# Picking the sixteen largest scores inside the query loop of a product-key mixer

## Chip, cores, metric

One Trainium2 chip, one core of it. The metric is the time of one execution on the device, in microseconds (us); lower is better. The engines are named as in the profile: PE (TensorE matmul), PEld (its weight loads), DVE (VectorE), ACT (ScalarE), POOL (GpSimd, which here also issues the indirect DMAs) and SP (which issues most plain DMAs).

## What is computed

One layer of a hybrid decoder for 1024 prompt tokens and 64 sample tokens, width 1024: RMSNorm, an input projection, retention and RWKV-7 mixing, an output projection, then a PEER product-key mixer, a gated per-layer embedding and a last RMSNorm. The change lies in PEER:

```python
q = (xb @ wq).reshape(PEER_BLOCK, PEER_HEADS, 2, PEER_DKEY // 2)
s = jnp.einsum('phcd,hcnd->phcn', q, keys).astype(jnp.float32)   # 8 heads x 2 halves x 128 scores
sv, si = lax.top_k(s, PEER_TOPK)                                  # 16 largest of each head half
cand = sv[:, :, 0, :, None] + sv[:, :, 1, None, :]
cv, ci = lax.top_k(cand.reshape(PEER_BLOCK, PEER_HEADS, PEER_TOPK * PEER_TOPK), PEER_TOPK)
e = (jnp.take_along_axis(si[:, :, 0], ci // PEER_TOPK, axis=-1) * PEER_NKEYS
     + jnp.take_along_axis(si[:, :, 1], ci % PEER_TOPK, axis=-1))
gsm = jax.nn.softmax(cv, axis=-1)
hval = jnp.einsum('pd,phkd->phk', xb, u_tab[e])
act = (jax.nn.gelu(hval.astype(jnp.float32), approximate=False) * gsm).astype(xb.dtype)
return jnp.einsum('phk,phkd->pd', act, v_tab[e])                  # 16384 experts
```

Each token has 16 head halves with 128 scores each; of every half the 16 largest are found, and of their sums the 16 best pairs of each of 8 heads, so 128 experts for a token.

## The kernel before

Tokens are cut into nine tiles: 0 to 7 are 128 prompt tokens each, tile 8 the 64 sample tokens. PEER is done in two ways. The tiles E0 = 0, 1, 8 and G1 = 2, 3 are *gathered*: for each of a tile's 128 expert slots (64 for tile 8, whose tokens fill the partitions twice) POOL issues an indirect DMA that fetches one row of 4 KB for each of 128 partitions into a buffer `grow` (L1127), and DVE multiplies it with the token's row and sums (L1141, first table, `in_pu`) or scales and adds it to `gacc` (L1155, second table, `in_pv`). These steps form one long chain, tile after tile. The tiles G2 = 4 to 7 are *dense*: all 16384 experts are multiplied on PE (`hidden`, L1256; `dense`, L1285), and a matrix of gate weights, made by `gates` (L1227) out of one-hot tiles `oh` (DVE L1242, ACT L1244, PE `pwt` L1247, ACT L1248), picks out the 128 that count.

A product of f32 quality is made of three float32r matmuls (`mm3`, L323: high x high, high x low, low x high), so each weight tile is first split in a high part (ACT, L297) and a low part (DVE L299 or POOL L301).

The program is written in one order, and a scheduler that simulates the engines turns it into one fixed instruction list for each engine: what was written earlier goes first when it is ready in the simulation. On the chip each engine works through its list in order, waiting on semaphores.

Written in this order, around the change:

1. `early` (L1211): queries, picks and gathers of E0, advanced a step at a time while the mixers run. What is left of it is written after the joint query (`run(early)`, L1489).
2. `c_query` (L1005), the joint query of G1 and G2: for each of the 16 head halves `hc` the query weights are loaded (`wqr`, L1012) and split (`wqh`, `wql`, L1015: low part on DVE for even `hc`, on POOL for odd), the projection `pq` of G1 (256 tokens) and of G2 (512 tokens) is made by 24 matmuls each, copied to `qT` (L1023), multiplied with the keys (`psc`, L1026), and the scores are copied to the tile `ss` (L1027). `ss` holds two halves and has one buffer for each of the two groups; after each odd `hc` it is written to DRAM (`sd`, L1030, six DMAs on ACT's queue for two halves).
3. `topk` (L1033) for each tile: the scores of all 16 halves are read back in one DMA (`s`, L1038, one buffer), and for each half five DVE instructions find the 16 largest and their places (L1043 to L1047). Then come the candidate sums, the second pick of 16 out of 50 for each of 8 heads (L1069 to L1073), and the look-up of the expert numbers (L1082 DVE, L1083 POOL, L1084 DVE).
4. The loop L1509: step `i` writes `topk` of the i-th tile of G2 alternately with `gates` of the tile before, then a fifth of 96 `hidden` blocks. `topk` and `gather` of tile 2 follow in step 1, those of tile 3 in step 4.
5. `dense_fused` and `dense_stored` (L1307, L1326), and then `ple` (L1373), which ends the program tile by tile in the order E0, G2, G1; a gathered tile's result comes back from DRAM there (`py`, L1390).

Of the kernel before, what the change touches and what calls it, by code (L numbers as in the profile page):

```python
# [8 lines left out]
F32 = mybir.dt.float32  # L9
# [3 lines left out]
U32 = mybir.dt.uint32  # L13
AF = mybir.ActivationFunctionType
# [164 lines left out]
G1 = [2, 3]  # L179
# [11 lines left out]
G2 = [4, 5, 6, 7]  # L191
RSTART = 2
RRATE = 1
ERATE = 1
QB = 4
EB = 150
SIZE = {t: (64 if t == 8 else 128) for t in range(9)}


def spans(tiles):  # L200

    e = [sum(SIZE[t] for t in tiles[:i]) for i in range(len(tiles) + 1)]
    return dict(zip(tiles, e)), e[-1]
# [8 lines left out]
class K:  # L212
# [434 lines left out]
    def group_b(self, tiles, early):  # L647
# [3 lines left out]
        with ExitStack() as e:  # L651
# [12 lines left out]
            for i, t in enumerate(tiles + [None]):  # L664
# [4 lines left out]
                while live or cur is not None:  # L669
# [9 lines left out]
                    for _ in range(ERATE if E0[1] in self.rowed else 0):  # L679
                        if steps < EB:  # L680
                            steps += 1
# [13 lines left out]
    def rw_mix(self, t):  # L695
# [282 lines left out]
        if t == 7:  # L978
            self.tail = self.ep0.tile([128, 512], F32, name="tail", tag="Wq", bufs=QB)
            nc.vector.tensor_tensor(self.tail, xf, p, op=OP.mult)  # L980
# [24 lines left out]
    def c_query(self, wp, da, parts):  # L1005

        nc, I = self.nc, self.I
        for hc in range(16):
            kT = wp.tile([128, 128], F32, name="keysT")
            nc.sync.dma_start(kT, I['keysT'][:, hc])  # L1010
            raw = da.tile([128, 8, 128], F32, name="wqr", tag="uraw", bufs=UB)
            nc.sync.dma_start(raw, I['wq'][hc])  # L1012
            wh = da.tile([128, 8, 128], F32R, name="wqh", tag="uh", bufs=DW)
            wl = da.tile([128, 8, 128], F32R, name="wql", tag="ul", bufs=DW)
            self.split(wh, wl, raw, "g" if hc % 2 else "v")  # L1015
            if hc % 2 == 0:
                st = [wp.tile([128, len(tiles), 2, 128], F32, name=f"ss{tiles[0]}", bufs=1) for tiles, _ in parts]
            for (tiles, x), s in zip(parts, st):
                off, n = spans(tiles)
                p = self.ps("pq", "b")  # L1020
                self.mm3(p[:, :n], lambda k: wh[:, k, :], lambda k: wl[:, k, :], lambda k: x[0][:, k], lambda k: x[1][:, k], 8)
                qT = wp.tile([128, n], F32, name=f"qT{tiles[0]}", bufs=1)
                nc.scalar.activation(qT, p[:, :n], AF.Copy)  # L1023
                p = self.ps("psc", "a")
                for i, t in enumerate(tiles):
                    nc.tensor.matmul(p[:SIZE[t], i * 128:i * 128 + 128], qT[:, off[t]:off[t] + SIZE[t]], kT, start=True, stop=True)  # L1026
                nc.scalar.activation(s[:, :, hc % 2], p[:, :len(tiles) * 128].rearrange("p (t k) -> p t k", k=128), AF.Copy)  # L1027
                if hc % 2:
                    for i, t in enumerate(tiles):
                        nc.scalar.dma_start(self.sd[t][:SIZE[t], hc - 1:hc + 1], s[:SIZE[t], i])  # L1030
            yield

    def topk(self, tp, t, s=None, tags={}, ce=None):  # L1033
        nc = self.nc
        n = SIZE[t]
        if s is None:
            w = tp.tile([128, 16, 128], F32, name="s", bufs=1)
            nc.sync.dma_start(w[:n], self.sd[t][:n])  # L1038
            s = [w[:, j] for j in range(16)]
        sv = tp.tile([128, 16, 16], F32, name="sv")  # L1040
        si = tp.tile([128, 16, 16], U32, name="si")
        for hc in range(16):
            nc.vector.max(sv[:n, hc, 0:8], s[hc][:n])  # L1043
            nc.vector.max_index(si[:n, hc, 0:8], sv[:n, hc, 0:8], s[hc][:n])
            nc.vector.match_replace(s[hc][:n], sv[:n, hc, 0:8], s[hc][:n], -3.0e38)
            nc.vector.max(sv[:n, hc, 8:16], s[hc][:n])
            nc.vector.max_index(si[:n, hc, 8:16], sv[:n, hc, 8:16], s[hc][:n])  # L1047
            yield
        sf = tp.tile([128, 8, 2, 16], F32, name="sf")
        nc.vector.tensor_copy(sf[:n].rearrange("p h c k -> p (h c) k"), si[:n])  # L1050
        nc.vector.tensor_scalar(sf[:n, :, 0], sf[:n, :, 0], 128.0, None, op0=OP.mult)
# [120 lines left out]
    def early_query(self, wp, t, wtag, wbufs, stags):  # L1172
# [31 lines left out]
        for j in range(2):  # L1204
            s.append(wp.tile([128, 8, 128], F32, name="es", tag=stags[j], bufs=QB if stags[j] == "Wq" else 1))
            nc.sync.dma_start(s[j][:n], self.sd[t][:n, 8 * j:8 * j + 8])
        yield
        ce = wp.tile([128, 2, 8, 50], F32, name="ce", tag="Wq", bufs=QB)
        yield from self.topk(wp, t, [s[j // 8][:, j % 8] for j in range(16)], dict(eq=dict(tag="xT")), (ce[:, 0], ce[:, 1]))

    def early(self, wp):  # L1211
# [4 lines left out]
        for t in E0[1:]:  # L1216
            while t not in self.rowed:
                next(g, None)
                yield
            for _ in self.early_query(wp, t, "Wq", QB, ("Wq", "xT")):  # L1220
                next(g, None)
# [200 lines left out]
    def build(self):  # L1422
# [3 lines left out]
        with self.es:  # L1426
# [21 lines left out]
            self.ep0 = ep0 = sb("early", ee, side="right")  # L1448
            self.layout(ep0, [("V", [128, D], F32, 2), ("W", [128, D], F32, 1), ("xy", [128, D], F32, 1), ("Wq", [128, D], F32, QB), ("xT", [128, D], F32, 1)])
            early = self.behind(self.early(ep0), PE_)  # L1450
# [4 lines left out]
            for _ in a:  # L1455
                for _ in range(IE):
# [3 lines left out]
            em.close()  # L1460
            cq = sb("cq", ew, bufs=2, side="right")
            parts = [G1, G2]
            self.layout(cq, [(f"ss{g[0]}", [128, len(g), 2, 128], F32, 1) for g in parts] +
                        [(f"qT{g[0]}", [128, spans(g)[1]], F32, 1) for g in parts])
            cn = sb("cn", ew, side="right")
            c1 = sb("cx1", ew, side="right")
# [2 lines left out]
            x = self.rows_of(cx, G2)  # L1469
            da = sb("dna", eg, bufs=2)  # L1470
            self.layout(da, [("uh", [128, 8, 128], F32R, DW), ("ul", [128, 8, 128], F32R, DW), ("uraw", [128, 8, 128], F32, UB)])
            tp = sb("tk", et)
            self.e12 = {}
            n3 = spans(G2[:-1])[1]
            query = self.c_query(cq, da, [(G1, x1), (G2, x)])
# [78 lines left out]
```

## Time and profile before

| what | value |
|---|---|
| median of 3 runs (lowest to highest) | 3917.6 us (3916.54 to 3927.6) |
| profiled execution | 3925.23 us, span 3923.2 us |
| busy share | PE 86%, DVE 77%, PEld 71%, POOL 60%, ACT 31% |
| mean granted PE clock | 0.875 |
| memory traffic | 279 GB/s over the span |

A row of the profile gives line, engine, operation, the tiles written and read, shapes and a count, then busy us, mean ns of one, and the idle time of that engine just before such instructions with what ended it. PE's busy time counts overlapping matmuls once, and a matmul's duration is longer than the distance to the next one.

### The profile page before, as it was taken

The page shows a single profiled execution, that of the slowest core. Times are in us where ns is not written, and L with a number is a line of the kernel's source. Part 1 is how long each engine was busy: PE and PEld are TensorE (multiplying, and loading weights), DVE is VectorE, ACT ScalarE, POOL GpSimd, SP SyncE. Part 2 cuts the span into 40 slices and gives each one's busy share as a digit, 9 for nine tenths or more (in the row PEclk, how much of TensorE's full clock was granted, in tenths as well). Part 3 has the DMA queues.
Part 4 walks back from the last instruction along what each step waited for, and adds up shares of the span by engine and source line. Part 5 has one row for each costly group of instructions (what it writes and reads, how often), then busy time and mean ns, then how long its engine had stood idle before and what let it go on. Part 6 is the DMA issues. An engine that isn't in the chain of part 4 may idle for free. (4 is left out here: it accounts for less than half of the span.)

```text
span 3923.2 us, 52738 instructions
## 1 busy us (share of the span) xinstructions
PE 3364.1 (86%) x17749; PEld 2766.9 (71%) x17749; DVE 3004.0 (77%) x5892; ACT 1225.6 (31%) x2247; POOL 2342.8 (60%) x2051
## 2 busy tenths in 40 slices
PE   8789995777869868875998899998799989899969
PEld 7688994545747756754887777787688767677757
DVE  4454487877896798876579999998877877888765
ACT  4232221111111111211322445678523333333322
POOL 5263175554364465554577778885588778887720
PEclk9799995667877658776999999999799999999989
DMA  7266558899778878888997788888999999999952
GB/s 256 68 226 207 169 198 276 273 303 307 226 243 278 297 257 273 294 300 311 321 350 259 241 289 291 326 313 327 335 342 344 333 354 357 370 367 348 327 177 72
DMA packets 465096, 1098.81 MB, mean 280 GB/s; under 512 B 74491, under 2 KB 183289, under 8 KB 459386
## 3 DMA queue, kind: packets, MB, share of 16 engines
q0 software_dynamic: 165888, 604.05, 43.9%
q1 hardware_dynamic: 237502, 389.07, 30.4%
q10 hardware_dynamic: 61436, 102.33, 7.0%
q8 instruction: 141, 2.31, 0.2%
q14 instruction: 129, 1.06, 0.1%
HBM read 992.98 MB, written 102.24 MB: 279 GB/s over the span
## 5 line engine op out<-in xcount | busy, mean ns | idle before, releaser
L1127 POOL DMA_INDIRECT grow<-in_pv,eid x576 | 573.5, 996 | 536.7 <-DVE gacc L1155 342.6
L1127 POOL DMA_INDIRECT grow<-in_pu,eid x576 | 573.9, 996 | 452.3 <-DVE grow L1141 277.8
L1155 DVE SCALAR_TENSOR_TENSOR gacc<-grow,ac,gacc 128x1024 f32<-128x1024 f32 x571 | 731.9, 1282 | 73.3 <-DMA grow<-in_pv,eid 68.8
L1141 DVE SCALAR_TENSOR_TENSOR grow<-grow,gacc 128x1024 f32<-128x1024 f32 x576 | 691.5, 1212 | 121.4 <-DMA grow<-in_pu,eid 100.7
L1300 PE MATMUL py<-ah,vl 128*128 128x512 f32 x1024 | 405.9, 402 | 31.7 <-POOL vl L301 31.4
L1300 PE MATMUL py<-ah,vh 128*128 128x512 f32 x1024 | 409.2, 400 | 18.2 <-ACT vh L297 18.1
L328 PE MATMUL ph<-cx,ul 128*128 128x512 f32 x1024 | 407.1, 398 | 9.2 <-POOL ul L301 9.2
L326 PE MATMUL ph<-cx,uh 128*128 128x512 f32 x1024 | 408.7, 399 | 7.0 <-ACT uh L297 5.3
L327 PE MATMUL ph<-cx,uh 128*128 128x512 f32 x1024 | 407.4, 398 | 0.0
L1300 PE MATMUL py<-al,vh 128*128 128x512 f32 x1024 | 405.1, 396 | 0.0
L301 POOL TENSOR_TENSOR vl<-vraw,vh 128x640 fp32r<-128x640 f32 (+2 forms) x224 | 325.6, 1459 | 42.7 <-ACT vh L297 36.7
L301 POOL TENSOR_TENSOR ul<-uraw,uh 128x1024 fp32r<-128x1024 f32 x128 | 307.9, 2406 | 35.2 <-ACT uh L297 32.8
L297 ACT ACTIVATE vh<-vraw 128x640 fp32r<-128x640 f32 (+2 forms) x224 | 154.8, 693 | 373.6 <-PE py L1300 165.5
L1300 PEld LDWEIGHTS py<-ah,vl 128*128 128x128 f32 x1024 | 193.3, 189 | 95.0 <-POOL vl L301 52.8
L1300 PEld LDWEIGHTS py<-ah,vh 128*128 128x128 f32 x1024 | 194.4, 190 | 77.1 <-ACT vh L297 36.5
L1304 DVE TENSOR_TENSOR yT<-yT,py 128x512 f32<-128x512 f32 x216 | 147.4, 684 | 121.7 <-PE py L1300 121.4
L328 PEld LDWEIGHTS ph<-cx,ul 128*128 128x128 f32 x1024 | 196.3, 192 | 51.4 <-POOL ul L301 10.9
L326 PEld LDWEIGHTS ph<-cx,uh 128*128 128x128 f32 x1024 | 196.1, 191 | 48.8 <-ACT uh L297 6.5
L327 PEld LDWEIGHTS ph<-cx,uh 128*128 128x128 f32 x1024 | 196.2, 192 | 40.3
L1300 PEld LDWEIGHTS py<-al,vh 128*128 128x128 f32 x1024 | 193.8, 189 | 43.1
L1247 PE MATMUL pwt<-oh,oh 128*128 128x128 f32 x1024 | 162.0, 310 | 63.2 <-ACT oh L1244 53.8
L1247 PEld LDWEIGHTS pwt<-oh,oh 128*128 128x128 f32 x1024 | 149.7, 213 | 84.7 <-ACT oh L1244 74.0
(401 smaller groups left out, 7815.1 us busy)
## 6 DMA issues: line engine op xcount, KB each, us to landing
uraw<-in_puT SPq DMA_DIRECT2D x128, 512.0 KB, 5.0
vraw<-in_pvd SPq DMA_DIRECT2D x152, 320.0 KB, 5.9
cw<-in_w_out SPq DMA_DIRECT2D x128, 256.0 KB, 5.5
wd<-wst ACTq DMA_DIRECT2D x28, 1024.0 KB, 15.4
wt<-wd SPq DMA_DIRECT2D x64, 448.0 KB, 7.5
wraw<-in_w_ret SPq DMA_DIRECT2D x48, 512.0 KB, 5.0
ewq<-in_wq SPq DMA_DIRECT2D x48, 512.0 KB, 5.5
gd<-geh ACTq DMA_DIRECT2D x96, 256.0 KB, 4.9
```

The lines of the kernel that those rows point to most:

```text
L297: nc.scalar.activation(hi, src, AF.Copy)
L301: nc.gpsimd.tensor_tensor(lo, src, hi.bitcast(F32), op=OP.subtract)
L326: mm(out, lh(k), rh(k), start=first and k == 0, stop=False)
L327: mm(out, lh(k), rl(k), start=False, stop=False)
L328: mm(out, ll(k), rh(k), start=False, stop=last and k == nk - 1)
L1127: nc.gpsimd.indirect_dma_start(out=g, out_offset=None, in_=src, in_offset=bass.IndirectOffsetOnAxis(ap=self.eid[t][:, j:j + 1], axis=0))
L1141: nc.vector.scalar_tensor_tensor(g[:, c], g[:, c], 1.0, x[:, c], op0=OP.mult, op1=OP.mult, accum_out=hv[:, i, j:j + 1])
L1155: nc.vector.scalar_tensor_tensor(y[:, c], g[:, c], ac[:, j:j + 1], y[:, c], op0=OP.mult, op1=OP.add)
L1247: nc.tensor.matmul(pw[:, j, :], oh[1][:, j, :], oh[0][:, j, :], start=True, stop=True)
L1300: nc.tensor.matmul(p, lh[:, b, :], rh, start=b == 0 and j == 0, stop=b == nb - 1 and j == 2)
L1304: nc.vector.tensor_tensor(yT[:, d, :], yT[:, d, :], p, op=OP.add)
```

## The change

`c_query` keeps one head half in an `ss` tile, with SB = 3 buffers for each group instead of one of double size. Right after the copy of the scores it runs the five pick instructions for each of the six tiles on `ss` (new method `pick`) and writes values and places into two tiles `sv`, `si` for each token tile (`self.found`), made before the query in the pool `tk`. The DMAs to `sd` are gone for these tiles. `topk` of the six tiles starts from `self.found`: it has no read-back, and its sixteen pick steps, each of which gave way to `gates`, are gone. The low part `wql` is made on POOL for every `hc`. For E0 nothing changes but the place of the five lines.

```diff
+SB = 3
@@ c_query
-            self.split(wh, wl, raw, "g" if hc % 2 else "v")
-            if hc % 2 == 0:
-                st = [wp.tile([128, len(tiles), 2, 128], F32, name=f"ss{tiles[0]}", bufs=1) for tiles, _ in parts]
-            for (tiles, x), s in zip(parts, st):
+            self.split(wh, wl, raw, "g")
+            for tiles, x in parts:
                 off, n = spans(tiles)
+                s = wp.tile([128, len(tiles), 128], F32, name=f"ss{tiles[0]}", bufs=SB)
...
-                nc.scalar.activation(s[:, :, hc % 2], p[:, :len(tiles) * 128].rearrange("p (t k) -> p t k", k=128), AF.Copy)
-                if hc % 2:
-                    for i, t in enumerate(tiles):
-                        nc.scalar.dma_start(self.sd[t][:SIZE[t], hc - 1:hc + 1], s[:SIZE[t], i])
+                nc.scalar.activation(s, p[:, :len(tiles) * 128].rearrange("p (t k) -> p t k", k=128), AF.Copy)
+                for i, t in enumerate(tiles):
+                    self.pick(self.found[t], hc, s[:, i], 128)
             yield
+
+    def pick(self, found, hc, s, n):
+        nc = self.nc
+        sv, si = found
+        nc.vector.max(sv[:n, hc, 0:8], s[:n])
+        nc.vector.max_index(si[:n, hc, 0:8], sv[:n, hc, 0:8], s[:n])
+        nc.vector.match_replace(s[:n], sv[:n, hc, 0:8], s[:n], -3.0e38)
+        nc.vector.max(sv[:n, hc, 8:16], s[:n])
+        nc.vector.max_index(si[:n, hc, 8:16], sv[:n, hc, 8:16], s[:n])
@@ topk
         if s is None:
-            w = tp.tile([128, 16, 128], F32, name="s", bufs=1)
-            nc.sync.dma_start(w[:n], self.sd[t][:n])
-            s = [w[:, j] for j in range(16)]
-        sv = tp.tile([128, 16, 16], F32, name="sv")
-        si = tp.tile([128, 16, 16], U32, name="si")
-        for hc in range(16):
-            (the same five instructions, then yield)
+            sv, si = self.found[t]
+        else:
+            sv = tp.tile([128, 16, 16], F32, name="sv")
+            si = tp.tile([128, 16, 16], U32, name="si")
+            for hc in range(16):
+                self.pick((sv, si), hc, s[hc], n)
+                yield
@@ build
-            self.layout(cq, [(f"ss{g[0]}", [128, len(g), 2, 128], F32, 1) for g in parts] +
+            self.layout(cq, [(f"ss{g[0]}", [128, len(g), 128], F32, SB) for g in parts] +
...
             tp = sb("tk", et)
+            self.found = {t: (tp.tile([128, 16, 16], F32, name=f"sv{t}"), tp.tile([128, 16, 16], U32, name=f"si{t}")) for t in G1 + G2}
```

More of the change, by code (lines that the diff above doesn't have):

```diff
@@ L1036, in topk @@
         if s is None:
-            w = tp.tile([128, 16, 128], F32, name="s", bufs=1)
-            nc.sync.dma_start(w[:n], self.sd[t][:n])
-            s = [w[:, j] for j in range(16)]
-        sv = tp.tile([128, 16, 16], F32, name="sv")
-        si = tp.tile([128, 16, 16], U32, name="si")
-        for hc in range(16):
[L1043 to L1048, printed above, removed]
+            sv, si = self.found[t]
[5 more added lines that the diff above has]
+                yield
         sf = tp.tile([128, 8, 2, 16], F32, name="sf")
```

## The prediction

> **What bounds the kernel now.** The page first: PE and DVE are both full, and fetches of 524 KB (604.05 MB by 2 x 576) use most of the memory traffic.
>
> ```profile
> span 3923.2 us, 52738 instructions
> PE 3364.1 (86%) x17749; PEld 2766.9 (71%) x17749; DVE 3004.0 (77%) x5892; ACT 1225.6 (31%) x2247; POOL 2342.8 (60%) x2051
> q0 software_dynamic: 165888, 604.05, 43.9%
> L1127 POOL DMA_INDIRECT grow<-in_pv,eid x576 | 573.5, 996 | 536.7 <-DVE gacc L1155 342.6
> ```
>
> A share is a mean over stages, so the windows come next: the query (1845 to 1998, where PE runs through), the stretch in which gates are made (2018 to 2797, its last 100 us also alone), the dense stretch, the hand-over to the last stage.
>
> ```profile
> core 0: us, PE busy (x) PEld busy (x) DVE busy (x) ACT busy (x) POOL busy (x), PEclk, DMA share, GB/s
> 1845.00:1998.00 153.00, 150.42 (x915) 133.03 (x914) 91.42 (x112) 46.35 (x80) 89.47 (x78) 1.00 0.94 335
> ...
> 2018.00:2797.00 779.00, 692.49 (x3334) 578.36 (x3332) 742.86 (x1981) 441.23 (x855) 553.59 (x408) 0.94 0.84 296
> 2700.00:2800.00 100.00, 59.83 (x305) 53.37 (x304) 89.92 (x143) 80.67 (x191) 39.62 (x40) 0.74 0.87 317
> 2797.00:3745.00 948.00, 899.23 (x3770) 705.60 (x3770) 754.75 (x1099) 327.27 (x527) 756.22 (x632) 0.99 0.98 347
> 3745.00:3795.00 50.00, 22.34 (x88) 16.68 (x87) 28.88 (x31) 8.22 (x17) 9.57 (x14) 0.69 0.58 195
> ```
>
> Each stretch has its own limit. The query is PE's: 150.4 of 153 us, 9.56 us for each of 16 head halves, while DVE has 61.6 us free. The gate stretch is DVE's: 742.9 of 779, a density of 0.954, and PE loses time. The dense stretch is PE's again, with the DMA engines full (0.98). What PE waits for in the gate stretch:
>
> ```profile
> PE pwt L1247 <- ACT oh L1244: 53.8, 47, 5.2
> PE ph L328 <- POOL ul L301: 9.2, 4, 3.0
> PE pit L1232 <- DVE e L1115: 6.9, 1, 6.9
> ```
>
> The ACT step waits for one-hots that DVE makes; POOL is held by fetches whose buffers DVE frees late; `e` is the end of the first `topk`. So DVE stands behind all three. At the end no `hidden` block is left and PE only follows the gates (59.8 us busy in 100, clock 0.74). The change takes DVE work out of this stretch and puts it where DVE has room: a gain as large as that room, if PE's query loop isn't held up.
>
> **The change part by part.** *The picks* (96 times five instructions) leave the gate stretch:
>
> ```profile
> L1141 DVE SCALAR_TENSOR_TENSOR grow<-grow,gacc 128x1024 f32<-128x1024 f32 x148 | 177.1, 1209 | 9.9 <-DMA grow<-in_pu,eid 9.8
> L1155 DVE SCALAR_TENSOR_TENSOR gacc<-grow,ac,gacc 128x1024 f32<-128x1024 f32 x72 | 91.7, 1274 | 0.2
> L1047 DVE FIND_INDEX8 si<-sv,s 128x8 uint32<-128x128 f32 x96 | 26.4, 281 | 0.0
> L1044 DVE FIND_INDEX8 si<-sv,s 128x8 uint32<-128x128 f32 x96 | 26.2, 282 | 0.0
> L1045 DVE MATCH_REPLACE8 s<-sv,s 128x128 f32<-128x128 f32 x96 | 25.8, 273 | 0.0
> L1046 DVE MAX8 sv<-s 128x8 f32<-128x128 f32 x96 | 24.0, 277 | 0.0
> L1043 DVE MAX8 sv<-s 128x8 f32<-128x128 f32 x96 | 21.3, 275 | 0.0
> L1045 DVE MATCH_VALUE_LOAD s<-sv,s 128x8 f32 x96 | 7.0, 73 | 0.0
> ```
> ```profile
> 2018.19 1.25 DVE L1043 MAX8 sv<-s 128x8 f32<-128x128 f32 x6
> ...
> 2024.81 0.08 DVE L1044 MATCH_VALUE_LOAD si<-sv,s 128x8 f32 x1
> 2024.88 0.28 DVE L1044 FIND_INDEX8 si<-sv,s 128x8 uint32<-128x128 f32 x1
> 2025.08 0.07 DVE L1044 MATCH_VALUE_LOAD si<-sv,s 128x8 f32 x1
> ```
>
> In the timeline picks of different halves are interleaved: a maximum takes 0.20 us of the queue (1.25 by 6), a load with its search 0.27 (2024.81 to 2025.08). One pick is 2 x 0.20 + 3 x 0.27 = 1.21 us, all 96 are 116 us. Chained, each waiting for the last, the full durations count: 275 + 277 + 282 + 273 + 281 + 3 x 73 ns = 1.61 us, 154 in all. Six tiles are ready at about the same time, so I take 1.21: 7.3 us per half (9.6 chained, the upper end).
>
> *What shares DVE with them in the query* is the gather of E0 and eight `wql`:
>
> ```profile
> L1155 DVE SCALAR_TENSOR_TENSOR gacc<-grow,ac,gacc 128x1024 f32<-128x1024 f32 x48 | 61.8, 1288 | 34.4 <-DMA grow<-in_pv,eid 33.8
> L1141 DVE SCALAR_TENSOR_TENSOR grow<-grow,gacc 128x1024 f32<-128x1024 f32 x45 | 54.2, 1220 | 39.9 <-DMA grow<-in_pu,eid 37.2 <-ACT gacc L1135 2.3
> L299 DVE TENSOR_TENSOR wql<-wqr,wqh 128x1024 fp32r<-128x1024 f32 x8 | 9.8, 1221 | 9.4 <-ACT wqh L297 6.0 <-PE ewo L602 3.3
> ```
>
> These rows cover 1805 to 2018: 93 steps in 213 us, 4.2 per half or 67 over sixteen. A step is 1.25 us of work (116.0 by 93) and 0.80 us of waiting for its fetch (74.3 by 93), 2.05 in all. Beside 7.3 us of picks in 9.56 there is room for 1.1 steps. The remaining E0 steps are written behind the query, so the fixed order should prefer picks; steps still fill holes that exist only in the simulation, so I take 1.5 (ends 1 and 4.2). Then a half takes 7.3 + 3.1 = 10.4 us and the query grows by 0.8 x 16 = **13 us**; 67 - 24 = 43 steps, 54 us of DVE, are put off. Three `ss` buffers let PE run two halves ahead, so single late fetches cost nothing.
>
> *The gate stretch* then has 742.9 - 116 + 54 = 681 us of DVE, at the same density 714 us: **65 us** shorter. PE's floor there:
>
> ```profile
> L326 PE MATMUL ph<-cx,uh 128*128 128x512 f32 x766 | 306.5, 400 | 7.0 <-ACT uh L297 5.3 <-ACT geh L1267 1.8
> L1247 PE MATMUL pwt<-oh,oh 128*128 128x128 f32 x1024 | 162.0, 310 | 63.2 <-ACT oh L1244 53.8 <-ACT wst L1248 5.7 <-DVE oh L1242 2.1
> ```
> ```profile
> 1959.70 0.39 PE L326 MATMUL pq<-cx,wqh 128*128 128x512 f32 x1
> 1959.92 0.39 PE L327 MATMUL pq<-cx,wqh 128*128 128x512 f32 x1
> 1960.16 0.40 PE L328 MATMUL pq<-cx,wql 128*128 128x512 f32 x1
> ...
> 1971.13 1.05 PE L1026 MATMUL psc<-keysT,qT 128*128 128x128 f32 x8
> ```
>
> 3 x 766 matmuls at 0.23 us apart are 529, 1024 small ones at 0.13 (1.05 by 8) are 134: 663, with some 30 us of waits 693. DVE's 714 still decides.
>
> *`wql` on POOL.* Eight more at the duration below, 19 us, in a stretch where POOL was busy 89 of 153; beyond that, fewer fetches are issued. Four buffers give slack; I cost it nothing. It is queued behind fetches that wait for DVE, which matters for the second rival.
>
> ```profile
> L301 POOL TENSOR_TENSOR wql<-wqr,wqh 128x1024 fp32r<-128x1024 f32 x8 | 19.1, 2383 | 3.5 <-ACT wqh L297 3.4
> L1038 SPq DMA_DIRECT2D s<-sd x6: 326/327/327, 2003.8 to 2343.2; - x6
> 1962.81 2.29 ACTq L1030 DMA_DIRECT2D sd<-ss  x4
> ```
>
> *The DRAM trip.* 96 writes on ACT's queue (2.29 us for four, some 55 us) and six read-backs on SP's go. ACT isn't what the query waits for, so the writes give nothing. The first read-back is issued at 2003.8 and the first pick starts at 2018.2; gather steps cover it partly, and its price is inside DVE's density. 12.6 MB fewer are moved (six tiles of 1.05 MB, out and back). The read-backs' single buffer and the sixteen steps shared with `gates` go too, which lets the first gates start some 50 to 80 us earlier (an estimate from 1.61 us x 16 and the 14 us of read-back); that alone moves no end, since DVE's sum decides.
>
> *The end.* The gather chain ends 37 us behind the dense stretch, and its last result is fetched only later:
>
> ```profile
> L1160 ACTq DMA_DIRECT2D yd<-gy x5: 326/326/326, 1256.3 to 3781.9; - x5
> L1390 SPq DMA_DIRECT2D py<-yd x6: 320/440/2342, 3748.3 to 3867.6; - x6
> ```
>
> From 3781.9 to 3867.6 there are 86 us of cover for put-off steps. I take **6 us** for fetches that now disturb the start of the last stage, where PE already idles 28 of 50 us (ends 0 and 40).
>
> Sum: -65 + 13 + 6 = **-46 us**. The profiled execution took 3925.2, 7.6 above the median, so 3879 against it, and 3917.6 - 46 = **3872** as the median.
>
> **The rivals.** *All of it fits (D):* no growth of the query, the gate stretch at PE's floor of 693: -86, **3832**. For it speaks DVE's free 61.6 us; against it, that the picks need twice that.
>
> *The query becomes DVE's (B, slower):* the fixed order keeps 4.2 gather steps between the picks of a half. Then a half takes 7.3 + 8.6 = 15.9 us, the query grows by 102, nothing is put off, the gate stretch falls to PE's floor (-86): +16, and with PE idling at each half some 10 more: **3944**. It decides from about 3.7 steps a half, or 2.6 if the picks run chained (9.6 + 5.3 = 14.9, +86). For it: the order is fixed, every late fetch stops the picks behind it, and POOL's fetches stand before `wql`. A clock that falls with idling is in the rows (0.74 where PE was 60% busy, 1.00 in the query). The Trainium skill, "TensorE: Matmul & The Clock Gate", Part 1, says that an idle window of about 3.4 us takes the clock to a half and that as much busy time brings it back; by that rule sixteen waits would cost up to 16 x 1.7 = 27 us instead of 10 (an estimate), and those rows agree with it.
>
> *The gather chain becomes last (C):* none of the 43 steps is made up, and a gate stretch 65 us shorter carries 18 fewer (220 in 779 us): 61 x 1.5 us (524 KB at 347 GB/s) = 93 us later against the dense end, 130 where 122 (3867.6 - 3745) are covered: 8 us, and with fetches through half of the last stage some 40 instead of 6: -65 + 13 + 8 + 40, **3914**. For it speaks a DMA share of 0.98 in the dense stretch, which leaves no room there. The Trainium skill, "Perfetto Trace Analysis", Engine Utilization, gives 358 GB/s as a core's memory peak; by it 347 leaves 11 GB/s, 20 steps in 948 us (an estimate), and the row's share of 0.98 agrees.
>
> **How the numbers follow.** The forecast 0.50, D 0.14, C 0.14, B 0.22. B has a real chance because the fixed order isn't visible in this trace. 0.3% is 12 us, about the spread of the runs. Faster: the forecast but for 0.02, D, and a quarter of C: 0.65; same: the rest of C and that 0.02: 0.13; slower: B, 0.22. The range runs from just below D to short of B, 3826 to 3938; the forecast's own reaches from 3866 (nothing lost at the end) to 3909 (picks chained: 9.6 + 3.1 = 12.7 us a half, the query grows by 50 instead of 13).
>
> **What would show it.** Right: PE runs through the query at a period of 9.6 to 10.6 us, DVE there above 0.9; the first `pit` before 2150; the stretch from query to first `py` shorter by some 50 to 80 us; the 100 us at clock 0.74 mostly gone. Wrong: a query period above 12 us with PE waiting on `qT`, `psc` or `wql` behind DVE (B); `yd` of the last tile within 60 us of the end (C).

## The result and the profile after

| | before | after |
|---|---|---|
| median (lowest to highest), 5 runs each | 3916.5 us (3914.5 to 3927.6) | 3879.1 us (3862.8 to 3893.6) |
| profiled execution, its span | 3925.2, 3923.2 us | 3881.5, 3879.7 us |
| mean granted PE clock | 0.875 | 0.883 |

The ratio is 0.9903, with an interval of 0.9874 to 0.9932: the kernel became 37 us faster where 46 were forecast, 7 us from the 3872 predicted. The sum was less right than its total, though. The profiled pair differs by 43.5 us of span, and four stretches can be cut out of it. They are bounded by three rows of each kernel: the last `psc` ends the query, the first `py` begins the dense stretch, and the last `py` ends it (columns: durations min/median/max in ns, first and last start in us). The five executions of after lie 31 us apart, so a difference of some 10 us between single stretches carries little. Two rows of before, then four of after:

```profile
L1026 PE MATMUL psc<-keysT,qT x192: 270/275/422, 1845.5 to 1998.5; 128*128 128x128 f32 x192
L1300 PE MATMUL py<-ah,vh x1024: 387/389/792, 2803.6 to 3745.2; 128*128 128x512 f32 x171
```
```profile
L1026 PE MATMUL psc<-keysT,qT x192: 270/275/377, 1844.3 to 1995.8; 128*128 128x128 f32 x192
L1235 PE MATMUL pit<-csta,e x8: 272/273/447, 2135.7 to 2658.5; 128*128 128x128 f32 x8
L1303 PE MATMUL py<-ah,vh x1024: 387/389/793, 2754.7 to 3705.2; 128*128 128x512 f32 x171
L1163 ACTq DMA_DIRECT2D yd<-gy x5: 326/326/333, 1257.7 to 3762.3; - x5
```

| stretch | before | after | difference | forecast |
|---|---|---|---|---|
| to the last `psc` | 1998.5 | 1995.8 | -2.7 | +13 |
| gates: last `psc` to first `py` | 805.1 | 758.9 | -46.2 | -65 |
| dense: first to last `py` | 941.6 | 950.5 | +8.9 | 0 |
| from there to the end of the span | 178.0 | 174.5 | -3.5 | +6 |
| sum | 3923.2 | 3879.7 | -43.5 | -46 |

The windows of after (span, then busy us and instruction count of PE, PEld, DVE, ACT and POOL, granted clock, DMA share, GB/s) show the query, the whole gate stretch, its last 100 us, the dense stretch and the hand-over:

```profile
1845.00:1998.00 153.00, 151.21 (x918) 134.15 (x917) 150.70 (x718) 47.08 (x80) 80.58 (x63) 1.00 0.71 227
1996.00:2755.00 759.00, 696.32 (x3414) 577.05 (x3412) 672.52 (x1389) 446.62 (x866) 586.74 (x435) 0.97 0.90 315
2654.70:2754.70 100.00, 77.16 (x410) 66.43 (x409) 79.00 (x134) 79.70 (x182) 49.85 (x42) 0.87 0.91 334
2747.00:3705.00 958.00, 901.31 (x3774) 707.45 (x3774) 757.07 (x1104) 325.46 (x528) 757.34 (x634) 0.99 0.98 345
3705.00:3755.00 50.00, 26.18 (x110) 20.24 (x109) 36.70 (x40) 7.99 (x16) 20.38 (x23) 0.76 0.84 268
```

DVE went from 91.4 to 150.7 us of the query's 153 and PE did not notice: 151.2 us busy at full clock. For the gate stretch the same window of before, on the same bounds, is

```profile
1998.00:2804.00 806.00, 712.87 (x3418) 595.20 (x3416) 759.06 (x2005) 450.78 (x868) 572.41 (x422) 0.94 0.84 297
```

DVE gave up 87 us there (759.1 to 672.5), but the stretch became only 47 us shorter: DVE's density fell from 0.942 to 0.886. What PE waits for in the gate stretch of after, and one line of DVE's own waits:

```profile
PE pwt L1250 <- ACT oh L1247: 30.8, 35, 3.7
PE ph L329 <- POOL ul L302: 14.3, 13, 3.4
PE pit L1235 <- DVE e L1118: 4.0, 1, 4.0
DVE oh L1245 <- PE pwt L1250: 42.9, 28, 4.5
```

PE's wait for one-hots fell from 53.8 to 30.8 us; its wait for `ul` on POOL rose from 9.2 to 14.3. The last line grew: DVE waits 42.9 us for PE to release one-hot buffers. In before it was

```profile
DVE oh L1242 <- PE pwt L1247: 23.2, 20, 3.4
```

So DVE no longer leads this stretch alone; more than before, the two wait for each other inside `gates`, which has two buffers of each `oh` tile. That this loop took up the other 40 us of the relief is read from these waits; no run gave it more buffers, so it is not shown.

### The profile page after: what moved, and what is told of

It reads as the page before. It is cut to its first block, busy times and chain, and to the rows that moved or that the text cites. A ratio compares the mean times of both kernels' runs of the same rounds, so it can differ in the third digit from the quotient of the medians.

```text
span 3879.7 us, 52665 instructions
## 1 busy us (share of the span) xinstructions
PE 3346.4 (86%) x17749; PEld 2748.3 (71%) x17749; DVE 2984.9 (77%) x5884; ACT 1220.5 (31%) x2247; POOL 2361.5 (61%) x2059
## 4 chain that ended last, share of the span: by engine, by line
PE 37%; DVE 24%; DMA 12%; POOL 8%; issue 8%; ACT 3%; ACTq 0%; SPq 0%; POOLq 0%; DVEq 0%
PE py L1303 13%; DVE grow L1144 6%; POOL grow L1130 4%; DMA grow<-in_pu,eid 4%; DVE gacc L1158 3%; DMA grow<-in_pv,eid 3%; PE ph L327 2%; PE ph L329 2%; PE ph L328 2%; POOL vl L302 2%; PE epq L1198 2%; DMA ft<-fd 2%; DVE eq L1085 2%; PE ewo L612 2%; DVE oh L1245 1%
## 5 line engine op out<-in xcount | busy, mean ns | idle before, releaser
L1144 DVE SCALAR_TENSOR_TENSOR grow<-grow,gacc 128x1024 f32<-128x1024 f32 x576 | 690.3, 1213 | 87.8 <-DMA grow<-in_pu,eid 77.2
L329 PE MATMUL ph<-cx,ul 128*128 128x512 f32 x1024 | 406.5, 398 | 14.4 <-POOL ul L302 14.3
L298 ACT ACTIVATE uh<-uraw 128x1024 fp32r<-128x1024 f32 x128 | 135.2, 1057 | 286.9 <-DMA uraw<-in_puT 144.3
L1245 DVE TENSOR_TENSOR oh<-csta,pit 128x512 f32<-128x512 f32 x256 | 162.3, 679 | 43.1 <-PE pwt L1250 42.9
```

Source lines behind the costliest of these rows:

```text
L298: nc.scalar.activation(hi, src, AF.Copy)
L329: mm(out, ll(k), rh(k), start=False, stop=last and k == nk - 1)
L1144: nc.vector.scalar_tensor_tensor(g[:, c], g[:, c], 1.0, x[:, c], op0=OP.mult, op1=OP.mult, accum_out=hv[:, i, j:j + 1])
L1245: nc.vector.tensor_tensor(oh[j], io, p[:, j, s + b:s + b + 4, None].to_broadcast([128, 4, 128]), op=OP.is_equal)
```

## The experiments

Edits are against the changed kernel unless the text says that they are against the kernel before. Ratios are to runs of before on the same chip in the same job. Stage times are cut as in the table above, from one profiled execution of each kernel. The first `psc` lies between 1825.5 and 1852.5 us in them, so lengths of stretches are compared, not the times at which they end.

**Which tiles' picks count.** Two kernels pick only one group of tiles in the loop, `G1` (tiles 2, 3) or `G2` (4 to 7); the other group keeps its DMAs to `sd` and picks in `topk`.

```diff
+PICKED = [G1]        # the other kernel: [G2]; a read-back in two halves of 4 KB there
-                s = wp.tile([128, len(tiles), 128], F32, name=f"ss{tiles[0]}", bufs=SB)
+                if tiles in PICKED:
+                    s = wp.tile([128, len(tiles), 128], F32, name=f"ss{tiles[0]}", bufs=SB)
+                elif hc % 2 == 0:
+                    held = wp.tile([128, len(tiles), 2, 128], F32, name=f"ss{tiles[0]}", bufs=1)
...
-                    self.pick(self.found[t], hc, s[:, i], 128)
+                    if tiles in PICKED:
+                        self.pick(self.found[t], hc, s[:, i], 128)
+                    elif hc % 2:
+                        nc.scalar.dma_start(self.sd[t][:SIZE[t], hc - 1:hc + 1], held[:SIZE[t], i])
```

> Picks inside the query loop for tiles 2 and 3 only (32 of 96); tiles 4 to 7 keep the trip through DRAM and their picks in topk. The time before is 3916.5 us, with all six tiles in the loop 3879. Theory 'relief' (the gain is DVE work, some 116 to 125 us, taken out of the stretch in which DVE sets the pace and put into DVE's idle time in the query): a third of the gain, 3900 to 3908. Rival 'sooner' (the gain is that the first gates need no read-back and no picks ahead of them): no gain, 3912 to 3920, since the tiles that have gates are as before. Rival 'traffic' (the gain is the 12.6 MB less through DRAM): a third too.

> Picks inside the query loop for tiles 4 to 7 only (64 of 96); tiles 2 and 3 keep the trip through DRAM, read back in two halves of 4 KB. 'Relief': two thirds of the gain, 3888 to 3896. 'Sooner': the whole gain, 3875 to 3883. 'Traffic': two thirds.

Picks of `G1` alone gave 3875.9 us, ratio 0.9894 (0.9857 to 0.9931); of `G2` alone 3867.7, ratio 0.9872 (0.9821 to 0.9922). A third of the picks brings what all of them bring, and so do the other two thirds: both intervals hold the full change's 0.9903. None of the times that were expected came: both kernels are faster than every theory had them. The gate stretch is 771 us long with `G1` alone and 752 with `G2` alone; their windows (first `G1`, second `G2`):

```profile
1988.00:2759.00 771.00, 694.69 (x3416) 580.75 (x3414) 699.47 (x1745) 451.56 (x866) 559.95 (x415) 0.96 0.86 303
```
```profile
1996.00:2748.00 752.00, 694.48 (x3417) 582.23 (x3415) 670.87 (x1529) 447.24 (x864) 572.39 (x422) 0.96 0.88 312
```

Against the same stretch of before, DVE minus 60 us made it 35 shorter, minus 88 made it 54 shorter, and PE's busy time is 694 to 696 us in all three. The gain does not add over the tiles. Nor does DVE's busy time in the stretch follow the picks alone: the gather steps fill it too, 229 of them in before, 222 with `G1` alone, 230 with `G2` alone, 243 in after.

**The load put back.** Here `topk` runs the five instructions again for each half, on other data and into tiles that nobody reads, giving way to `gates` after each as before.

```diff
             sv, si = self.found[t]
+            flat = sv.rearrange("p a b -> p (a b)")
+            for hc in range(16):
+                (tiles again, againv, againi)
+                (the five instructions on x = flat[:, 8 * hc:8 * hc + 128])
+                yield
```

> The changed kernel, and in topk of each of the six tiles the sixteen picks are run a second time on the found values, with their results unused: the DVE work of before is back in the gate stretch, without the trip through DRAM, and nothing waits for it. 'Relief': the gain is gone, 3905 to 3930, gate stretch (last query matmul to first dense output) back at 770 to 800 us. 'Traffic': the gain stays, 3875 to 3890. 'Sooner': most of it stays, 3880 to 3895, if the first gates still start by 2150.

3933.0 us, ratio 1.0039 (1.0017 to 1.0061): 54 us slower than the changed kernel. Its gate stretch is 821 us:

```profile
1993.00:2815.00 822.00, 716.88 (x3420) 596.68 (x3418) 789.01 (x2175) 450.81 (x865) 598.48 (x452) 0.93 0.86 301
PE pwt L1262 <- ACT oh L1259: 54.5, 43, 5.3
```

Density 0.960, clock 0.93, and the wait for one-hots at 54.5: the picture of before is back with the load alone. It is a little worse than in before, and past the expected 800 us, since the put-off gather steps lie in this stretch as well (259 against 229 in before). DVE's work in that stretch is the cause of the gain, and not the DRAM trip, which is left out here as in after. The rival by which the gain is an earlier start of the first gates ('sooner') is not settled by this run, whose first `pit` came at 2159.4, later than the 2150 that its test asked for.

**`wql` on POOL alone**, against the kernel before:

```diff
-            self.split(wh, wl, raw, "g" if hc % 2 else "v")
+            self.split(wh, wl, raw, "g")
```

> The kernel before with one edit: the low part of all sixteen query weight tiles on POOL. The runs with the picks of two, four and six tiles in the loop gained 40, 49 and 37 us and all contain this edit. Theory 'relief with a floor' (the gate stretch follows DVE's work in it down to a floor near 755 us that PE and the gates' own loop set): this edit takes no DVE work out of the gate stretch, so 3908 to 3920, gate stretch 795 to 810. Rival 'common edit' (what the three share is the cause, the number of picks moved is not): 3875 to 3890.

3910.7 us, ratio 0.9983 (0.9960 to 1.0006): nothing that can be told from no change, as the prediction had costed it. The gate stretch is 801 us long. This run also bears on 'sooner'. From the last `psc` to the first `pit` it is 187 us in before, 166 here, 166 with the load put back, 173 with `G1` alone and 140 in after; the gate stretches are 805, 801, 821, 771 and 759 us. Twenty us of earlier start brought 4 us of stretch here and none with the load put back, and a smaller one went with 34 us in `G1`. The start of the first gates does not set the length.

**Is the query near its limit?** Three kernels load it in different ways. In the first, four steps of the gather chain are written behind each query half, so that the program order asks for them there.

```diff
-            run(query)
+            for _ in query:
+                for _ in range(4):
+                    next(early, None)
```

> The changed kernel, with four steps of what is left of the early gathers written behind each head half of the query, where they stood behind the whole query. This is the slower rival of the prediction made on purpose: the fixed order then keeps about four gather steps among the picks of a half. If the order is what kept the query whole (DVE at 0.98 in it, PE undisturbed): the query grows by 60 to 100 us, the gate stretch becomes 20 to 35 us shorter, 3905 to 3950. If the three score buffers and the filling by readiness keep PE running whatever the order: 3870 to 3885.

3883.7 us, ratio 0.9912 (0.9882 to 0.9943). The query stayed whole, 151 us from the first `psc` to the last. The steps that DVE did in it are these, beside those of after in its query:

```profile
L1144 DVE SCALAR_TENSOR_TENSOR grow<-grow,gacc x14: 1202/1217/1228, 1962.4 to 2001.0; 128x1024 f32<-128x1024 f32 x14
L1158 DVE SCALAR_TENSOR_TENSOR gacc<-grow,ac,gacc x31: 1265/1279/1293, 1854.5 to 1956.4; 128x1024 f32<-128x1024 f32 x31
```
```profile
L1144 DVE SCALAR_TENSOR_TENSOR grow<-grow,gacc x15: 1217/1230/1241, 1954.2 to 1996.4; 128x1024 f32<-128x1024 f32 x15
L1158 DVE SCALAR_TENSOR_TENSOR gacc<-grow,ac,gacc x31: 1270/1283/1295, 1846.3 to 1948.2; 128x1024 f32<-128x1024 f32 x31
```

45 against 46. The scheduler's list did not take the steps, so this kernel does not test the rival it was made for. The second doubles four of the five pick instructions inside the loop:

```diff
                 for i, t in enumerate(tiles):
+                    (dv, di: tiles againv, againi, bufs=2)
+                    nc.vector.max(dv[:, 0:8], s[:, i])
+                    nc.vector.max_index(di[:, 0:8], dv[:, 0:8], s[:, i])
+                    nc.vector.max(dv[:, 8:16], s[:, i])
+                    nc.vector.max_index(di[:, 8:16], dv[:, 8:16], s[:, i])
                     self.pick(self.found[t], hc, s[:, i], 128)
```

> The changed kernel with four of each pick's five instructions run a second time on the same scores ahead of the pick, results unused: DVE's work in the query rises from about 7.8 to about 13.3 us a head half, where PE needs 9.6. If the query is held by DVE once the picks alone exceed PE's period, with three score buffers giving no more than a delay: the last score matmul 40 to 70 us later, PE waiting for score buffers, gathers of the early tiles nearly stopped in the query, time 3925 to 3960. If the fixed order lets the copies run on and picks pile up behind the query: the query whole, the gate stretch 40 to 80 us longer, 3915 to 3950. Where the time goes tells the two apart.

3993.9 us, ratio 1.0204 (1.0171 to 1.0238), slower than either expectation. Its query takes 293 us, with these windows (query, gate stretch) and this wait of PE in the query:

```profile
1832.00:2125.00 293.00, 178.82 (x917) 155.31 (x916) 291.52 (x1254) 49.45 (x81) 145.61 (x131) 0.77 0.74 241
2125.00:2876.00 751.00, 695.90 (x3443) 585.32 (x3443) 626.79 (x1445) 446.71 (x865) 526.55 (x384) 0.96 0.80 282
PE psc L1026 <- ACT ss L1027: 105.3, 14, 13.1
```

The query is now DVE's, and it grew by 141 us for 90 us of extra picks (96 x 2 x (0.20 + 0.27)): more gather steps came into it too, 113 of them against 46 in after, where the expectation had them nearly stopped. The gate stretch had 46 us less DVE work than after, and became 9 us shorter: 759 with 673 of DVE, 750 with 627. Less DVE work is worth little there. The third keeps the work and takes the slack away:

```diff
-SB = 3
+SB = 1
```

> The changed kernel with one buffer for the scores of each group instead of three, so a half's scores are copied only when the picks of the half before are done. Theory (the step in the prediction that three buffers cover late picks): DVE is 0.985 busy in the query, its picks lag, and PE waits for ACT's copies at many of the sixteen halves; the query grows by 20 to 60 us and most of it stays: 3895 to 3935. Rival: ACT waited for picks once only (4.8 us), the buffers are idle and nothing changes: 3870 to 3890.

3911.5 us, ratio 0.9999 (0.9976 to 1.0022): nearly the whole gain is gone. Its query and PE's wait in it:

```profile
1826.00:2056.00 230.00, 169.35 (x919) 147.86 (x918) 223.16 (x861) 49.24 (x82) 137.76 (x122) 0.84 0.85 287
PE psc L1026 <- ACT ss L1027: 55.2, 12, 11.3
ACT ss L1027 <- DVE si L1039: 69.3, 23, 9.3
```

In after ACT's copies waited for picks three times, 4.8, 2.5 and 1.3 us. DVE is nearly as full (223 of 230 us) as in after (150.7 of 153); what differs is whether a late pick stops the next copy. Read alone, a DVE share of 0.985 would have said that the query is DVE's in both kernels, and PE's wait says which one it is. The query grew by 78 us; the gate stretch, to which it left less DVE work, was 20 us shorter (739), the dense stretch 14 shorter (937). That is 44 us in all; the profiled execution lost 27, as its first `psc` came 18 us earlier (1826.6), ahead of anything that this edit touches.

**The DRAM trip.** One kernel writes each half's scores to `sd` after the picks, 96 DMAs, and `topk` also reads them back in four pieces, with a one-column copy on POOL so that something waits for them. A second one only writes.

```diff
                     self.pick(self.found[t], hc, s[:, i], 128)
+                    nc.scalar.dma_start(self.sd[t][:, hc], s[:, i])
...
             sv, si = self.found[t]
+            for k in range(4):                      # not in the second kernel
+                w = tp.tile([128, 4, 128], F32, name="s", bufs=1)
+                nc.sync.dma_start(w, self.sd[t][:, 4 * k:4 * k + 4])
+                nc.gpsimd.tensor_copy(w[:, 0, 0:1], w[:, 3, 0:1])
```

> The changed kernel with the trip through DRAM back in it: after its pick each score tile is written to DRAM (96 DMAs on ACT's queue), and topk of each tile reads the 1 MB back in four pieces, of which POOL copies one column so that the reads are waited for; the picks stay where they are. Theory 'relief': the trip is worth little, 3875 to 3895. Rival 'traffic': the gain is gone, 3900 to 3920.

> The changed kernel, and the scores of each half are also written to DRAM as soon as the picks are done (96 writes on ACT's queue, nothing is read back). It parts the 18 us that writes and read-backs together cost. If the writes carry it (ACT's time in the query, 6.3 MB): 3892 to 3900. If the read-backs do (their waits on POOL, single buffer): 3874 to 3886.

With writes and read-backs: 3897.5 us, ratio 0.9962 (0.9946 to 0.9977), between the two expectations. With writes alone: 3880.5, ratio 0.9899 (0.9852 to 0.9946). The writes cost nothing, although 96 DMAs are twice what the kernel before issued. The other 17 us (25 by the two ratios, which are from different jobs) come with the read-backs as made here. At least part of them sits in the gate stretch, 781 us long where it is 770 with writes alone, though its first `pit` came at 2120.3, 15 us before that of after. PE's waits there:

```profile
PE pwt L1255 <- ACT oh L1252: 33.7, 32, 3.1
PE ph L329 <- POOL ul L302: 25.6, 15, 3.8
```

PE's wait for `ul` from POOL is 25.6 us where it was 14.3 in after and 15.0 with writes alone, and POOL carries the copies that wait for the read-backs. In the kernel before, nothing on POOL waited for them, so these 17 us are no price of the trip that the change removed; that price was not isolated.

**The hole at the end of the gate stretch.** In the last 100 us before the first `py` PE works 57.7 us in before (59.8 in the window of the prediction, which ends 4 us earlier) and 77.2 in after, since the 96 `hidden` blocks (`NPRE`) have run out: their last matmul starts at 2697.9 in before and 2711.0 in after. Eight more of them were put there, and so taken out of the dense stretch: in the changed kernel, in the kernel before, and in the version with picks of `G2` alone.

```diff
-NPRE = 96
+NPRE = 104
```

> The changed kernel with 104 instead of 96 hidden blocks written among the gates (the other 24 are fused into the dense stretch). Theory of the floor: after the change the gate stretch is no longer DVE's, it ends with the last tile's gates, about 96 us behind the last pit, and in its last 100 us PE has 82 us of work at clock 0.90 because the hidden blocks have run out; eight more blocks fill that hole and leave the dense stretch. The gate stretch grows by some 35 us, the dense stretch shrinks by some 60, the time falls by 20 to 30 us: 3849 to 3860. Rival: the gain of the version with picks of tiles 4 to 7 alone (3842) comes from the picks that it leaves out of the query: then eight blocks do nothing here, 3872 to 3885.

> The kernel before with 104 instead of 96 hidden blocks among the gates, nothing else. Theory: the hole at the end of the gate stretch (59.8 us of PE in 100, clock 0.74) is there before the change too, so the blocks fill it and the time falls by 25 to 40 us, 3877 to 3892: the change is not needed for that gain, and the two gains add. Rival: DVE sets the end of the gate stretch there and the blocks' own gate products lengthen it, so the gain needs the change: 3905 to 3920.

> Picks in the loop for tiles 4 to 7 only, which ran 3867.7 us, and 104 instead of 96 hidden blocks made and stored in the gate stretch. If that stretch's floor is the gates' own loop, with PE idle about 55 us in it, eight more blocks of 5.5 us on PE fill the idle time and the dense stretch gets 44 us shorter: 3830 to 3860. If ACT, POOL and the DMA engines have no room for them, the stretch grows by as much: 3862 to 3885.

| kernel | `NPRE` 96 | `NPRE` 104 | ratio of the latter to before |
|---|---|---|---|
| before | 3917.4 | 3882.5 | 0.9908 (0.9874 to 0.9941) |
| changed | 3879.1 | 3843.2 | 0.9800 (0.9751 to 0.9849) |
| `G2` alone | 3867.7 | 3842.4 | 0.9839 (0.9805 to 0.9873) |

The changed kernels' medians come from different jobs, the ratios from one job each. 35 us without the change and 36 with it: the two gains add (0.9903 by 0.9908 is 0.981, and 0.980 was measured). `G2` alone gained 25. Two of the three times lie in the range that was expected, and the changed kernel's is 6 us below it. The last 100 us and PE's wait for one-hots, of the changed kernel with 104 blocks:

```profile
2688.00:2788.00 100.00, 82.82 (x440) 71.03 (x439) 73.66 (x107) 68.95 (x140) 64.32 (x50) 0.93 0.94 340
PE pwt L1250 <- ACT oh L1247: 19.1, 24, 2.6
```

and the stretches, gates and dense, of the same kernel:

```profile
1987.00:2788.00 801.00, 742.75 (x3655) 616.39 (x3654) 695.61 (x1418) 463.98 (x886) 621.36 (x459) 0.98 0.90 316
2788.00:3670.00 882.00, 841.28 (x3541) 662.17 (x3539) 704.43 (x1049) 311.34 (x501) 702.04 (x582) 0.99 0.98 350
```

The gate stretch grew by 43 us (802 from 759), the dense stretch lost 72 (878 from 950.5, first `py` to last). These two kernels, at 3843 and 3842 us, beat both the kernel before and the changed one; which of the two is better is not settled.

## Why the prediction was right, and where its steps were off

**Right: the mechanism and the bound.** The gate stretch shrank because DVE lost work there, which the load put back showed; `wql` on POOL cost nothing; the writes gave nothing; and the last `yd` left at 3762.3, 117 us ahead of the end, so the gather chain did not become last. It trails the last `py` by 57 us instead of 37, so it lost 20 us where that rival had 93. The 358 GB/s by which the rival left so little room in the dense stretch is no limit here: the page of before has slices of 370 and 367 GB/s in it. Three of the signs came as written: a query period of 9.7 us (`psc` of two successive halves starts at 1881.19 and 1890.89) with DVE above 0.9, the first `pit` at 2135.7, and the last 100 us of the gate stretch at clock 0.87 instead of 0.74. The fourth, a stretch 50 to 80 us shorter, was missed narrowly at 46. (The period was 9.7 in before too, 1882.37 to 1892.07; the prediction's 9.56 divides by sixteen a window that is a little shorter than sixteen halves.)

**Mis-sized: the gate stretch, -65 forecast, -46 measured.** Two steps failed there in opposite directions. DVE's sum was put at minus 62 us (116 out, 54 in) and was minus 87: only 14 more gather steps lie in the stretch (243 against 229), where 43 were to come in; the picks that trail into it add some 18 us (10 to 20 of each of the five instructions at 0.20 and 0.26 us). Then that sum was divided by the old density of 0.954, "at the same density", which holds only as long as DVE alone sets the pace; even at the top of the table below, 30 us of DVE were worth 16. The check against "PE's floor" of 693 us did not catch it, because that floor was too low. On nearly the prediction's bounds (22 us after the last `psc` to 8 before the first `py`) after has

```profile
2018.00:2747.00 729.00, 672.74 (x3312) 557.61 (x3311) 643.34 (x1274) 437.24 (x852) 568.34 (x421) 0.98 0.91 318
```

PE is busy for 673 us where the prediction counted 663 from four matmul groups, and idle for 56 where it put "some 30 us of waits". The term that was too small is above all the waits, 26 us short, which are mostly those for one-hots and for `ul` shown above. The rows over the kernels, from the last `psc` to the first `py` (26 us more than the prediction's bounds in before), busy times from windows rounded to a microsecond:

| kernel | DVE busy in the gate stretch | its length | PE busy |
|---|---|---|---|
| load put back | 789 | 821 | 717 |
| before | 759 | 805 | 713 |
| `wql` alone | 753 | 801 | 708 |
| `G1` alone | 699 | 771 | 695 |
| writes alone | 686 | 770 | 700 |
| four gather steps written in | 673 | 763 | 694 |
| after | 673 | 759 | 696 |
| `G2` alone | 671 | 752 | 694 |
| writes and read-backs | 666 | 781 | 704 |
| picks doubled | 627 | 750 | 696 |
| one buffer | 625 | 739 | 688 |

Between load put back and before 30 us of DVE cost 16; from before to after 87 bring 46; from after to the doubled picks or to one buffer some 47 bring 9 and 20. So a microsecond of DVE was worth about half of one down to some 670, and less below; no row shows a sharp floor, and the read-backs lie off this line. From the top of the table to the bottom PE's wait for one-hots falls from 54.5 to 20.3 us and DVE's wait for PE to release them rises from 18.3 to 42.8, which fits two engines that hold each other up. The rival in which all of it fits (3832) fell by this too: its 693 would be some 719 in this table, and the shortest row is 739.

**Mis-sized: the query, +13 forecast, none measured.** Two terms in it were off. The pick at 1.21 us held: independent searches follow at 0.26 us in after's timeline (1900.02 to 1900.28), maxima at 0.20. But the put-off steps were 23, not 43: 93 in the window from 1805 to 2018 before, 70 after,

```profile
L1158 DVE SCALAR_TENSOR_TENSOR gacc<-grow,ac,gacc 128x1024 f32<-128x1024 f32 x48 | 61.7, 1285 | 13.9 <-DMA grow<-in_pv,eid 13.3 <-DVE gacc L1158 0.3
L1144 DVE SCALAR_TENSOR_TENSOR grow<-grow,gacc 128x1024 f32<-128x1024 f32 x22 | 26.1, 1230 | 0.0
```

and a step cost 1.25 us, not 2.05. The 0.80 us of waiting for its fetch had been carried over from a loop in which DVE had nothing else to do; with picks to run meanwhile it went away (1.4 us between 1845 and 2018, where it was 63.3). And 7.3 + 46 by 16 x 1.25 = 10.9 us a half, above PE's 9.7, still held nobody up, since the picks may trail:

```profile
L1039 DVE FIND_INDEX8 si<-sv,ss x96: 287/301/310, 1848.4 to 2028.5; 128x8 uint32<-128x128 f32 x96
```

The last search starts 33 us after the last `psc`. Three buffers and the end of the loop absorb it; with one buffer the same kernel lost 32 us. "Three `ss` buffers let PE run two halves ahead" was the step on which the forecast stood.

**The rival of a query bound by DVE (3944)** did not come, but the mechanism is real: with one buffer and with doubled picks it came just as described, PE waiting on `psc` behind ACT behind DVE. Its price per wait can be read there. The same 917 to 919 matmuls kept PE busy for 178.8 us instead of 151.2 with doubled picks, 27.6 us for 14 waits or 2.0 each, and 169.4 with one buffer, 18.1 for 12 waits or 1.5 each, at clocks of 0.77 and 0.84. The Trainium skill, "TensorE: Matmul & The Clock Gate", Part 1, gave 1.7 us for a wait of over 3.4 us by the estimate in the prediction; these rows, 2.0 and 1.5, lie on both sides of it. The 10 us that the prediction took for the sixteen waits were too few.

**Not foreseen: +8.9 in the dense stretch.** PE's busy time in it is the same (899 and 900 us). What grew is its wait for `vl` from POOL, here in before and in after:

```profile
PE py L1300 <- POOL vl L301: 30.5, 32, 3.3
PE py L1303 <- POOL vl L302: 40.0, 46, 2.2
```

Its waits for `vh` from ACT inside the stretch are 11.2 and 9.5 us. Why POOL was later was not tested. Over the other kernels with 96 blocks that stretch varies between 937 and 952 us, in no order that the experiments explain; this stays open. **The end, +6 forecast, -3.5 measured:** the last stage did not get longer; the hand-over window has PE at 26.2 of 50 us, better than the 22.3 before.

**An error in the working.** "96 writes on ACT's queue, some 55 us" is wrong. Before issued 48, one for two halves of a tile, some 27 us by the same row:

```profile
L1030 ACTq DMA_DIRECT2D sd<-ss x48: 326/450/1315, 1859.3 to 2001.1; - x48
```

It did not enter the sum, as the writes were priced at nothing, and 96 writes turned out to cost nothing either.

So the total came close because a gate stretch 19 us too optimistic and a dense stretch 9 off met a query and an end that were 16 and 9 too pessimistic (-46 + 19 + 9 - 16 - 9.5 = -43.5). That these errors cancel is luck; that DVE's work in the gate stretch carried the gain is not.

## What to carry to other kernels

When work leaves the engine that leads a stretch, do not simply divide its new sum by the old density: here two engines waited for each other, and a microsecond taken from DVE was worth about half of one. Take the lower bound from the second engine's whole busy time in the stretch plus the waits that stay, which were the larger miss (56 us where 30 were put), and not from its largest instruction groups. Filler work that an engine does between fetches loses its waiting when other work is put beside it, so cost it at its work, and ask whether a loop has the buffers to let the new work trail: three buffers against one were worth nearly as much as the change (32 of 37 us). And a stretch in which the busiest engine runs out of independent work at the end (58 to 77 us in the last 100) may be cheaper to fill than to shorten: eight blocks moved there brought as much as this change did, with it or without.

## What the runs showed that was not expected

An engine 98% busy was no bound: DVE at 150.7 of 153 us held nothing up with three buffers, and at 223 of 230 held PE for 55 us with one. The pick instructions also took longer inside the query than in the `topk` of before, 299 ns for a search instead of 281, although their pitch was unchanged at 0.26 to 0.27 us:

```profile
L1036 DVE FIND_INDEX8 si<-sv,ss 128x8 uint32<-128x128 f32 x96 | 26.8, 299 | 0.0
```

With one buffer the same line measured 282. No experiment looked for the reason.
